# The low part of each weight tile in two pieces on GpSimd (one core, two hybrid layers with PEER experts)

## The chip, the cores and the metric

The kernel runs on one core of one Trainium2 chip. A core has five engines with an instruction stream each: TensorE (PE in the profile; its loads of weights are PEld), VectorE (DVE), ScalarE (ACT), GpSimd (POOL) and SyncE (SP). They wait for each other through semaphores. Transfers are carried out by 16 DMA engines, from queues that SyncE or GpSimd fill. The metric is the device time of one execution in microseconds; lower is better. Several runs of a kernel are compared by their median.

## The reference

Two layers of a diffusion trunk over 512 latent tokens and 256 context tokens, with 1024 channels. Each layer is a normalised and modulated mixer followed by a normalised and modulated expert stage (PEER). Layer 0 mixes by differential attention and a gated linear recurrence, layer 1 by a gated delta rule and windowed attention. After layer 0 the context is no longer needed. The expert stage of each layer matters most here:

```python
def peer_ffn(h, w_q, keys, u_tab, v_tab):          # P_HEADS 8, P_NKEYS 128, P_TOPK 16
    ...
    def block(xb):                                 # 128 tokens
        q = (xb @ w_q).reshape(P_TOKEN_BLOCK, P_HEADS, 2, P_DQ // 2)
        s = jnp.einsum('nhpd,hpkd->nhpk', q, keys).astype(jnp.float32)
        s_top, i_top = lax.top_k(s, P_TOPK)
        cand = (s_top[:, :, 0, :, None] + s_top[:, :, 1, None, :]).reshape(...)
        cand_idx = (i_top[:, :, 0, :, None] * P_NKEYS + i_top[:, :, 1, None, :]).reshape(...)
        best, pos = lax.top_k(cand, P_TOPK)
        idx = jnp.take_along_axis(cand_idx, pos, axis=-1)
        gate = jax.nn.softmax(best, axis=-1)
        u = u_tab[idx]
        v = v_tab[idx]
        act = jax.nn.gelu(jnp.einsum('nd,nhkd->nhk', xb, u).astype(jnp.float32), approximate=False)
        return jnp.einsum('nhk,nhkd->nd', (gate * act).astype(v.dtype), v)
```

The tables `u_tab` and `v_tab` have 16384 rows of 1024 numbers each per layer. Everything is computed in float32.

## The kernel before

**Products in three parts.** A float32 product is made from fp32r operands in three matmuls. Each operand x is split into a high part, a rounded copy that ScalarE makes (`activation ... Copy`, line 230), and a low part x - high (`tensor_tensor ... subtract`, line 233), on VectorE or GpSimd as the caller says. `mm3` then sums high by high (line 250), high by low (line 251) and low by high (line 253), for k = 0 to 7, one k after the other, 128 rows of the inner dimension at a time.

**Weight tiles.** `chunk` loads one weight tile of 128 x 1024 (`wraw`, 8 blocks k of 128 columns), and makes `whi` on ScalarE and `wlo` on GpSimd. A string `s.los` of letters says where the low part of the next tile is made, 'p' for GpSimd; only in the first, context stage every third one is VectorE's ('ppv', 10 tiles), everywhere else all are GpSimd's: 405 tiles, one of which has only 128 columns. The tiles are loaded ahead: `wraw` has two buffers, `whi` and `wlo` two (more in some stages).

**The stages**, in us of the profiled execution: the mixers of layer 0 and the context's retrieval to 960; the norm of layer 0's expert stage and its first query products to 1040; retrieval, expert inputs and spread of layer 0 to 1890; the sum over experts of layer 0 (`peer_out`) to 2880; layer 1's mixer to 3640; its norm and queries to 3777; retrieval, expert inputs and spread of layer 1 to 4500, of which up to 4168 mainly retrieval; `peer_out` of layer 1 to 5170; the final norm.

**Experts, dense and sparse.** Most tokens take a dense way: for each of 128 blocks j of the table, `expert_in` forms gelu(u_j . x) for all of them (matmuls `u`, lines 250, 251 and 253, with `hh` and `hl`, the parts of the normalised tokens), and `peer_out` multiplies by the gate matrix `G` and by the v rows. Ninety-six of the 128 blocks are made ahead, in `u_step` during retrieval and spread, and put aside in DRAM (`AD`); `u_step` splits its tiles two steps ahead. The last 32 are made in `peer_out`, with tiles loaded three ahead.

*Retrieval* (`retrieve`, `top`): per head two rounds of eight maxima with their indices for each of two halves, then sums of candidates `cd` (lines 1584 and 1586) and again top 16 of these, all on VectorE (lines 1553 to 1557 are the top-8 searches).

*Spread* makes the dense gate matrix: one-hot rows `ohA` (line 1685, VectorE) and `ohB` (line 1695 VectorE, 1692 and 1693 ScalarE, in turn for some tiles), a matmul `g` (line 1697) for each token, a copy `stg` to SBUF (1698) and a transfer to `G`.

*Sparse*: the remaining tokens (128 or 256 of them) get their rows by gathers. `fetch` (line 1721) is an indirect DMA that GpSimd issues, of 128 rows of 1024 numbers into a buffer `ga`; VectorE then makes a dot product (line 1733, `pu`) or a weighted sum (line 1746, `pv`) from each. There are 4 (layer 0) or 6 (layer 1) buffers, and one or two gathers are taken per step of the other work (`pull`).

**Order.** A scheduler with a timeline of its own sets the order of each engine's instructions from the program. A gather is put behind the last low part that GpSimd was given: `s.anchor` is that instruction, and `fetch` issues with `issue_after(s.anchor)`. So the low parts, the gathers and the other low parts on GpSimd (`hl` of the norm; `wl` of the gates in `peer_out`) share one queue whose order the scheduler chooses.

Of the kernel before, what the change touches and what calls it, by code (L numbers as in the profile page):

```python
# [9 lines left out]
F32 = mybir.dt.float32  # L10
# [4 lines left out]
AF = mybir.ActivationFunctionType  # L15
OP = mybir.AluOpType
# [4 lines left out]
DT = D // 128  # L21
# [186 lines left out]
class Net:  # L208
# [130 lines left out]
    def chunk(s, src):  # L339

        nc = s.nc
        r = s.t(s.next_pool(s.rps), [128, DT, 128], tag='wraw')
        up = s.next_pool(s.ups)
        hi = s.t(up, [128, DT, 128], F32R, tag='whi')
        lo = s.t(up, [128, DT, 128], F32R, tag='wlo')
        m = src.shape[2]
        nc.sync.dma_start(out=r[:, :, 0:m], in_=src)
        s.los = s.los[1:] + s.los[0]
        s.split(r[:, :, 0:m], hi[:, :, 0:m], lo[:, :, 0:m], lo_eng=nc.gpsimd if s.los[-1] == 'p' else nc.vector)
        return hi, lo  # L350


# [1714 lines left out]
```

## Time and profile before

| | |
|---|---|
| runs | 5204.75, 5197.26, 5203.47 us; median 5203.47 |
| profiled execution | 5212.4 us, its span 5210.6 us |
| busy share: PE, PEld, DVE, ACT, POOL | 86%, 70%, 77%, 39%, 53% |
| mean granted clock of TensorE | 0.92 |
| `wlo` on GpSimd (line 233) | 405 instructions, 1018.5 us busy, 2517 ns in the mean |
| waits of PE for `wlo` (line 253) | 116.2 us |
| gathers (line 1721) | 512 from `pu`, 384 from `pv`, 1313 and 1333 ns each on GpSimd |

Busy shares are means over stages with different limits. A wait is idle time of an engine that ended when the named instruction of another engine was done. "PE u L253 <- POOL wlo L233" reads: the matmul `u` of line 253 on TensorE waited for the low part `wlo` of line 233 on GpSimd.

### The profile page before, as it was taken

To read this page: it belongs to the slowest core of one execution; us is meant where nothing else is said; L and a number is where in the kernel's file an instruction comes from. 1 tells how busy PE (TensorE), PEld (TensorE's weight loads), DVE (VectorE), ACT (ScalarE), POOL (GpSimd) and SP (SyncE) were. 2 spreads that over 40 slices of the span, in tenths; PEclk is the share of its full clock that TensorE was granted. 3 is DMA by queue.
4 is the path that set the end of the run, shared out by engine and by line. 5 is a ranking of instruction groups with operands and counts; after the bars stand their busy time and mean duration, and the time that the engine had idled before them with its cause. 6 is when DMAs were issued, how large, how long until landed. Compare 5 with 4: busy or idle time off the path is not lost. (4 is left out here: it accounts for less than half of the span.)

```text
span 5210.6 us, 73804 instructions
## 1 busy us (share of the span) xinstructions
PE 4469.9 (86%) x26350; PEld 3651.6 (70%) x26350; DVE 4026.8 (77%) x7777; ACT 2019.6 (39%) x3979; POOL 2769.9 (53%) x1839
## 2 busy tenths in 40 slices
PE   7899988788889979999899898897966777799997
PEld 5777766576677867777677676785766676677775
DVE  4665568899999868888887774662699988788997
ACT  3444443234555642222222365342333553233332
POOL 2232223676557746655565320442466676587884
PEclk8899998898999989999999997898977888899999
DMA  5431124687778978887787310004367787899996
GB/s 200 145 115 60 59 77 154 196 270 239 248 264 294 321 275 298 291 296 273 279 286 274 113 51 25 6 6 145 103 219 232 254 291 266 292 343 330 356 353 218
DMA packets 453552, 1109.50 MB, mean 213 GB/s; under 512 B 40640, under 2 KB 204864, under 8 KB 449088
## 3 DMA queue, kind: packets, MB, share of 16 engines
q1 hardware_dynamic: 323872, 633.91, 36.2%
q0 software_dynamic: 129312, 470.87, 25.4%
q8 instruction: 208, 3.41, 0.3%
q14 instruction: 160, 1.31, 0.1%
HBM read 995.58 MB, written 109.05 MB: 212 GB/s over the span
## 5 line engine op out<-in xcount | busy, mean ns | idle before, releaser
L233 POOL TENSOR_TENSOR wlo<-wraw,whi 128x1024 fp32r<-128x1024 f32 x405 | 1018.5, 2517 | 1033.9 <-ACT whi L230 954.8
L1721 POOL DMA_INDIRECT ga<-in_pu,idx x512 | 672.3, 1313 | 380.9 <-DVE ga L1733 122.7
L253 PE MATMUL u<-hh,wlo 128*128 128x512 f32 (+1 forms) x2048 | 750.4, 367 | 116.2 <-POOL wlo L233 116.2
L1733 DVE SCALAR_TENSOR_TENSOR ga<-ga,htok 128x1024 f32<-128x1024 f32 x512 | 762.1, 1504 | 64.7 <-DMA ga<-in_pu,idx 64.5
L250 PE MATMUL u<-hh,whi 128*128 128x512 f32 (+1 forms) x2048 | 749.2, 366 | 45.5 <-DVE xl L1912 23.7
L251 PE MATMUL u<-hl,whi 128*128 128x512 f32 (+1 forms) x2048 | 739.9, 361 | 0.0
L230 ACT ACTIVATE whi<-wraw 128x1024 fp32r<-128x1024 f32 x415 | 436.8, 1054 | 739.2 <-PE u L251 350.8
L1746 DVE SCALAR_TENSOR_TENSOR sacc<-ga,sact,sacc 128x1024 f32<-128x1024 f32 x381 | 589.2, 1546 | 100.8 <-DMA ga<-in_pv,idx 89.0
L1721 POOL DMA_INDIRECT ga<-in_pv,idx x384 | 512.0, 1333 | 220.3 <-DVE sacc L1746 82.5
L253 PEld LDWEIGHTS u<-hh,wlo 128*128 128x128 f32 x2048 | 431.3, 211 | 164.6 <-POOL wlo L233 124.5
L250 PEld LDWEIGHTS u<-hh,whi 128*128 128x128 f32 x2048 | 431.8, 211 | 101.5 <-DVE xl L1912 34.2
L251 PEld LDWEIGHTS u<-hl,whi 128*128 128x128 f32 x2048 | 429.9, 210 | 39.2
L233 DVE TENSOR_TENSOR vl<-vraw,vh 128x768 fp32r<-128x768 f32 (+1 forms) x256 | 354.4, 1392 | 88.0 <-ACT vh L230 71.5
L1697 PE MATMUL g<-ohB,ohA 128*128 128x128 f32 x1792 | 300.7, 299 | 129.1 <-DVE ohB L1695 106.1
L1697 PEld LDWEIGHTS g<-ohB,ohA 128*128 128x128 f32 x1792 | 265.5, 205 | 176.6 <-DVE ohB L1695 76.8
L1695 DVE TENSOR_SCALAR ohB<-c_all,pt 128x128 f32<-128x128 f32 x512 | 314.4, 637 | 60.9 <-PE g L1697 60.5
L230 ACT ACTIVATE vh<-vraw 128x768 fp32r<-128x768 f32 (+1 forms) x256 | 239.6, 945 | 283.9 <-PE acc L1991 222.2
L1992 PE MATMUL acc<-wh,vl 128*128 128x512 f32 x768 | 305.9, 398 | 30.0 <-DVE vl L233 29.8
L1990 PE MATMUL acc<-wh,vh 128*128 128x512 f32 x768 | 292.8, 396 | 28.0 <-ACT wh L230 27.9
L1991 PE MATMUL acc<-wl,vh 128*128 128x512 f32 x768 | 302.5, 394 | 8.8 <-POOL wl L233 8.8
L2007 PE MATMUL acc<-vl,wh 128*128 128x512 f32 x768 | 256.6, 401 | 16.1 <-DVE vl L233 15.9
L2006 PE MATMUL acc<-vh,wh 128*128 128x512 f32 x768 | 222.5, 401 | 50.8 <-ACT vh L230 29.7
(513 smaller groups left out, 10099.2 us busy)
## 6 DMA issues: line engine op xcount, KB each, us to landing
wraw<-in_uT SPq DMA_DIRECT2D x256, 512.0 KB
vraw<-in_pv SPq DMA_DIRECT2D x256, 512.0 KB
G<-stg SPq DMA_DIRECT2D x28, 2048.0 KB
wraw<-in_ada_w SPq DMA_DIRECT2D x96, 512.0 KB
wraw<-in_ew SPq DMA_DIRECT2D x64, 512.0 KB
G<-G SPq DMA_DIRECT2D x32, 1024.0 KB
wraw<-in_pwq SPq DMA_DIRECT2D x48, 512.0 KB
AD<-act SPq DMA_DIRECT2D x96, 256.0 KB
```

Of the source, the lines that this page charges most:

```text
L230: nc.scalar.activation(hi, x, AF.Copy)
L233: i = (lo_eng or nc.vector).tensor_tensor(lo, x, hi.bitcast(F32), OP.subtract)
L250: nc.tensor.matmul(o, a, hh[:, k], start=(k == 0), stop=False)
L251: nc.tensor.matmul(o, a, hl[:, k], start=False, stop=False)
L253: nc.tensor.matmul(o, b, hh[:, k], start=False, stop=(k == nk - 1))
L1695: nc.vector.tensor_scalar(B, C['iota'], pt[:, 1, c:c + 1], pt[:, 2, c:c + 1], op0=OP.is_equal, op1=OP.mult)
L1697: nc.tensor.matmul(ps[:, n], A[:, n], B, start=True, stop=True)
L1721: nc.gpsimd.indirect_dma_start(out=ga, out_offset=None, in_=tab, in_offset=bass.IndirectOffsetOnAxis(ap=idx[:, k:k + 1], axis=0))
L1733: nc.vector.scalar_tensor_tensor(ga, ga, 1.0, htok, op0=OP.mult, op1=OP.mult, accum_out=act[:, k:k + 1])
L1746: nc.vector.scalar_tensor_tensor(acc, ga, act[:, k:k + 1], acc, op0=OP.mult, op1=OP.add)
L1991: nc.tensor.matmul(acc[d], a, wl, start=False, stop=False)
L1992: nc.tensor.matmul(acc[d], b, wh, start=False, stop=sp)
```

## The change

In `chunk`, where the low part is GpSimd's, it is made in two instructions of 4 blocks k, 512 columns each, instead of one of 8 blocks. The high part stays one instruction on ScalarE. `s.anchor` becomes the second of the two. Where the low part is VectorE's, nothing changes. Line numbers from 350 on move by 8; the new subtraction is on line 354 and its copy on 351.

```diff
--- before.py
+++ after.py
@@ -346,7 +346,15 @@
         m = src.shape[2]
         nc.sync.dma_start(out=r[:, :, 0:m], in_=src)
         s.los = s.los[1:] + s.los[0]
-        s.split(r[:, :, 0:m], hi[:, :, 0:m], lo[:, :, 0:m], lo_eng=nc.gpsimd if s.los[-1] == 'p' else nc.vector)
+        if s.los[-1] == 'p':
+
+            nc.scalar.activation(hi[:, :, 0:m], r[:, :, 0:m], AF.Copy)
+            for k in range(0, DT, DT // 2):
+                p = slice(k, k + DT // 2)
+                i = nc.gpsimd.tensor_tensor(lo[:, p, 0:m], r[:, p, 0:m], hi[:, p, 0:m].bitcast(F32), OP.subtract)
+            s.anchor = i.ins
+        else:
+            s.split(r[:, :, 0:m], hi[:, :, 0:m], lo[:, :, 0:m])
         return hi, lo
```

The order of all engines changes with it, since the scheduler gives each instruction its place. Three places follow, before and after the change; numbers in names differ by position only (`ga`: gather buffer, `wlo`: low part of a weight tile, `hl`: low part of the normalised tokens).

GpSimd at the norm of layer 0's expert stage, before the change:

```order
L1721 DMA ga_8449<-in_pu,idx_1732_8260 128x1024
L1721 DMA ga_8451<-in_pu,idx_1732_8260 128x1024
L1721 DMA ga_8453<-in_pu,idx_1732_8260 128x1024
L1721 DMA ga_8455<-in_pu,idx_1732_8260 128x1024
L233 TENSOR_TENSOR hl_8747<-h_8891,hh_8746 128x512
L233 TENSOR_TENSOR hl_8747<-h_8896,hh_8746 128x512
L233 TENSOR_TENSOR hl_8747<-h_8901,hh_8746 128x512
L1721 DMA ga_8458<-in_pu,idx_1732_8260 128x1024
L1721 DMA ga_8493<-in_pu,idx_1732_8260 128x1024
L233 TENSOR_TENSOR hl_8747<-h_8906,hh_8746 128x512
L1721 DMA ga_8496<-in_pu,idx_1732_8260 128x1024
L1721 DMA ga_8531<-in_pu,idx_1732_8260 128x1024
```

and after it:

```order
L233 TENSOR_TENSOR hl_8833<-h_8977,hh_8832 128x512
L233 TENSOR_TENSOR hl_8833<-h_8982,hh_8832 128x512
L233 TENSOR_TENSOR hl_8833<-h_8987,hh_8832 128x512
L1729 DMA ga_8528<-in_pu,idx_1732_8338 128x1024
L1729 DMA ga_8530<-in_pu,idx_1732_8338 128x1024
L1729 DMA ga_8532<-in_pu,idx_1732_8338 128x1024
L1729 DMA ga_8534<-in_pu,idx_1732_8338 128x1024
L233 TENSOR_TENSOR hl_8833<-h_8992,hh_8832 128x512
L233 TENSOR_TENSOR hl_8833<-h_8997,hh_8832 128x512
L1729 DMA ga_8537<-in_pu,idx_1732_8338 128x1024
L1729 DMA ga_8573<-in_pu,idx_1732_8338 128x1024
L1729 DMA ga_8576<-in_pu,idx_1732_8338 128x1024
```

Three `hl` now stand ahead of the four gathers that they stood behind, and the fourth `hl` stands behind four gathers instead of six.

GpSimd in the spread of layer 1, around the weight tiles 350 to 353, before the change (both pieces begin with the same gather, the 601st of the program):

```order
L1721 DMA ga_36305<-in_pu,idx_6889_33160 128x1024
L1721 DMA ga_36308<-in_pu,idx_6889_33160 128x1024
L233 TENSOR_TENSOR wlo_36596<-wraw_36594,whi_36595 128x1024
L1721 DMA ga_36372<-in_pu,idx_6889_33160 128x1024
L1721 DMA ga_36416<-in_pu,idx_6889_33160 128x1024
L233 TENSOR_TENSOR wlo_36669<-wraw_36667,whi_36668 128x1024
L1721 DMA ga_36419<-in_pu,idx_6889_33160 128x1024
L1721 DMA ga_36456<-in_pu,idx_6889_33160 128x1024
L233 TENSOR_TENSOR wlo_36745<-wraw_36743,whi_36744 128x1024
L1721 DMA ga_36514<-in_pu,idx_6889_33160 128x1024
L1721 DMA ga_36517<-in_pu,idx_6889_33160 128x1024
L233 TENSOR_TENSOR wlo_36818<-wraw_36816,whi_36817 128x1024
```

and after it ("x2" is two instructions that follow each other):

```order
L1729 DMA ga_36640<-in_pu,idx_6889_33442 128x1024
L354 TENSOR_TENSOR wlo_36936<-wraw_36934,whi_36935 128x512 x2
L1729 DMA ga_36643<-in_pu,idx_6889_33442 128x1024
L1729 DMA ga_36708<-in_pu,idx_6889_33442 128x1024
L354 TENSOR_TENSOR wlo_37010<-wraw_37008,whi_37009 128x512 x2
L1729 DMA ga_36753<-in_pu,idx_6889_33442 128x1024
L354 TENSOR_TENSOR wlo_37087<-wraw_37085,whi_37086 128x512 x2
L1729 DMA ga_36756<-in_pu,idx_6889_33442 128x1024
L1729 DMA ga_36794<-in_pu,idx_6889_33442 128x1024
L1729 DMA ga_36853<-in_pu,idx_6889_33442 128x1024
L354 TENSOR_TENSOR wlo_37161<-wraw_37159,whi_37160 128x512 x2
L1729 DMA ga_36856<-in_pu,idx_6889_33442 128x1024
```

The first `wlo` stands one gather earlier, the following ones one to two gathers earlier than before, counted from the same first gather.

TensorE in the spread of layer 1, around the weight tile 330, before the change, with what each row waits for (Pool_49 is GpSimd's semaphore):

```order
L1697 MATMUL g_34534<-ohB_34547,ohA_34535 128x128 [waits Activation_49]
L253 MATMUL u_35574<-hh_31545,wlo_35497 128x256 [waits Pool_49]
L250 MATMUL u_35574<-hh_31545,whi_35496 128x256
L251 MATMUL u_35574<-hl_31546,whi_35496 128x256
L253 MATMUL u_35574<-hh_31545,wlo_35497 128x256
```

and after it:

```order
L253 MATMUL u_35896<-hh_31806,wlo_35817 128x256 [waits Pool_49]
L250 MATMUL u_35896<-hh_31806,whi_35816 128x256
L251 MATMUL u_35896<-hl_31807,whi_35816 128x256
L253 MATMUL u_35896<-hh_31806,wlo_35817 128x256
...
L251 MATMUL u_35896<-hl_31807,whi_35816 128x256
L1705 MATMUL g_34782<-ohB_34785,ohA_34783 128x128 [waits DVE_49,Activation_49]
L1705 MATMUL g_34782<-ohB_34788,ohA_34783 128x128 [waits Activation_49]
L253 MATMUL u_35896<-hh_31806,wlo_35817 128x256 [waits Pool_49]
L250 MATMUL u_35896<-hh_31806,whi_35816 128x256
L251 MATMUL u_35896<-hl_31807,whi_35816 128x256
L253 MATMUL u_35896<-hh_31806,wlo_35817 128x256
```

There was one wait for GpSimd, at k = 0 (the first row of line 253); now there are two, at k = 0 and at k = 4, and two `g` matmuls (line 1705 after the change) stand between.

## Rows read from the trace of the kernel before

**Rows 1.** Three stretches; columns: stretch, length, busy us of PE, PEld, DVE, ACT, POOL, PEclk.

```profile
1040.00:1540.00 500.00, 428.45 (x2000) 351.02 (x1999) 490.42 (x1263) 224.66 (x458) 321.41 (x189) 0.94 0.77 254
3777.00:4168.00 391.00, 267.36 (x1723) 254.38 (x1722) 388.48 (x942) 157.00 (x311) 254.87 (x149) 0.79 0.74 235
4168.00:4500.00 332.00, 229.80 (x1435) 213.22 (x1435) 260.59 (x421) 134.07 (x271) 203.48 (x118) 0.82 0.77 269
```

**Rows 2.** GpSimd's work on wlo alone, in three stretches; x is the count of instructions.

```profile
1040.00:1540.00 500.00, 157.98 (x62) 0.94 0.77 254
3777.00:4168.00 391.00, 144.56 (x59) 0.79 0.74 235
4500.00:5170.00 670.00, 64.67 (x25) 0.98 0.95 340
```

**Rows 3.** Waits of PE, 3777 to 4168; columns: total us, times, longest us.

```profile
PE u L253 <- POOL wlo L233: 71.7, 18, 14.3
```

**Rows 4.** Waits of PE, 4168 to 4500.

```profile
PE u L253 <- POOL wlo L233: 42.4, 19, 5.8
PE g L1697 <- DVE ohB L1695: 29.1, 26, 3.0
```

**Rows 5.** Waits of DVE, 4168 to 4500.

```profile
DVE ohB L1695 <- PE g L1697: 45.3, 11, 9.1
```

**Rows 6.** Instructions of line 233 over the span: ns min/median/max, first and last start.

```profile
L233 POOL TENSOR_TENSOR wlo<-wraw,whi x405: 461/2398/3851, 40.9 to 5007.1; 128x1024 fp32r<-128x1024 f32 x135
L233 POOL TENSOR_TENSOR wl<-ad,wh x96: 1267/1297/2012, 1900.0 to 2873.8; 128x512 fp32r<-128x512 f32 x96
L233 POOL TENSOR_TENSOR wl<-G,wh x128: 986/1180/2377, 4496.2 to 5161.9; 128x384 fp32r<-128x384 f32 x128
```

**Rows 7.** Groups of DVE by line, 1040 to 1540: busy us, mean ns.

```profile
L1584 DVE TENSOR_TENSOR cd<-tv 128x64 f32<-128x64 f32 x29 | 23.0, 793 | 0.0
L1586 DVE TENSOR_TENSOR cd<-tv 128x48 f32<-128x48 f32 x29 | 11.8, 405 | 0.0
```

**Rows 8.** Groups of DVE by line, 3777 to 4168.

```profile
L1584 DVE TENSOR_TENSOR cd<-tv 128x64 f32<-128x64 f32 x20 | 23.9, 1195 | 0.0
L1586 DVE TENSOR_TENSOR cd<-tv 128x48 f32<-128x48 f32 x19 | 14.6, 766 | 0.0
```

**Rows 9.** Timeline, 3781 to 3783; columns: start us, us, engine, line.

```profile
3781.41 0.19 DVE L1586 TENSOR_TENSOR cd<-tv 128x48 f32<-128x48 f32 x1
3782.16 2.41 POOL L233 TENSOR_TENSOR wlo<-wraw,whi 128x1024 fp32r<-128x1024 f32 x1 [0.86 <-ACT whi L230]
3782.53 2.13 DVE L1584 TENSOR_TENSOR cd<-tv 128x64 f32<-128x64 f32 x1
```

**Rows 10.** Timeline, 4569 to 4574: two subtractions of GpSimd and a dot.

```profile
4569.03 2.56 POOL L233 TENSOR_TENSOR wlo<-wraw,whi 128x1024 fp32r<-128x1024 f32 x1
4569.27 3.41 DVE L1733 SCALAR_TENSOR_TENSOR ga<-ga,htok 128x1024 f32<-128x1024 f32 x1
4571.55 2.00 POOL L233 TENSOR_TENSOR wl<-G,wh 128x384 fp32r<-128x384 f32 x1
```

**Rows 11.** Timeline, 3845 to 3855, GpSimd and VectorE.

```profile
3845.74 8.40 DVE L1733 SCALAR_TENSOR_TENSOR ga<-ga,htok 128x1024 f32<-128x1024 f32 x1
3846.05 7.00 POOL L233 TENSOR_TENSOR wlo<-wraw,whi 128x1024 fp32r<-128x1024 f32 x3
```

**Rows 12.** Waits of DVE, 950 to 1000.

```profile
DVE h L305 <- POOL hl L233: 6.2, 1, 6.2
```

**Rows 13.** Timeline of GpSimd, 955 to 966.

```profile
956.27 1.11 POOL L1721 DMA_INDIRECT ga<-in_pu,idx  x1 [4.91 <-DVE idx L1711]
961.13 2.49 POOL L233 TENSOR_TENSOR hl<-h,hh 128x512 fp32r<-128x512 f32 x2
```

**Rows 14.** Timeline, 4211 to 4214.

```profile
4211.54 2.36 POOL L233 TENSOR_TENSOR wlo<-wraw,whi 128x1024 fp32r<-128x1024 f32 x1
4213.96 0.58 PE L253 MATMUL u<-hh,wlo 128*128 128x256 f32 x1 [2.21 <-POOL wlo L233]
```

## The prediction

> **What bounds the kernel now.** I read the busy time by stretches first, then the waits of TensorE and VectorE in the stretches where a low part is waited for, and last the timeline around single low parts. GpSimd itself bounds nothing: it is busy 53% of the span. Three places depend on when a low part (`wlo`) is ready, or on how long it holds up another engine.
>
> (a) The two stretches in which VectorE is the bound. From 1040 to 1540 (retrieval of layer 0) it is busy 490.42 of 500 us, from 3777 to 4168 (the same of layer 1) 388.48 of 391, while TensorE has 428.45 and 267.36 [rows 1]. TensorE does wait for `wlo` there, 71.7 us in 18 waits of layer 1 [rows 3], but those waits are bought with time that VectorE needs anyway, so shortening them ends nothing sooner. What counts is what VectorE loses to GpSimd. It loses much: the sum `cd` of 64 columns that a top-16 search begins with (L1584) takes 1195 ns in the mean from 3777 to 4168 [rows 8], and its short neighbour of 48 columns 0.19 us when nothing runs on GpSimd [rows 9]. One long `cd` begins 0.37 us into a `wlo` and ends with it: 2.13 us, from 3782.53 to 3784.66, where the `wlo` of 3782.16 ends at 3784.57 [rows 9]. So a VectorE instruction of this kind stands still until GpSimd's tensor operation is over.
>
> (b) The stretch from 4168 to 4500 (spread of layer 1). No engine is full there. TensorE waits 42.4 us in 19 waits for `wlo` and 29.1 us in 26 for the one-hot rows `ohB` of VectorE [rows 4]; VectorE in turn waits 45.3 us in 11 waits for the `g` matmuls of TensorE [rows 5]. This is a loop: VectorE frees a gather buffer, GpSimd issues the gather and then makes `wlo`, TensorE stands at the `u` matmul that needs `wlo` with `g` matmuls behind it, and VectorE waits for those. Here a low part that is usable sooner ends the stretch sooner.
>
> (c) The norm of layer 0, where VectorE waits 6.2 us once for an `hl` [rows 12], which GpSimd begins at 961.13, behind four gathers that start at 956.27 [rows 13].
>
> **The price of two pieces.** A `wlo` of 1024 columns takes 2.398 us in the median, a 512-column subtraction of the same kind (`wl<-ad`) 1.297 us [rows 6]. Two pieces: 2 x 1.297 = 2.59 us, so 0.20 us more per weight tile; by the shortest row of the 512-column form, 1.267, it is 2.53 and +0.14. I take +0.17. The first piece is ready 2.40 - 1.30 = 1.10 us sooner, the second 0.17 later. 404 tiles x 0.17 = 69 us of GpSimd's time, in the idle half of that engine except where VectorE or TensorE stands behind it.
>
> **Term 1, the norm of layer 0: -5 us.** The new order puts three `hl` ahead of the four gathers (the first place in the change's section). The wait of 6.2 us loses the 961.13 - 956.27 = 4.9 us of gathers. Bounds 0 (the gathers' later start costs it again) and -6.
>
> **Term 2, the VectorE-bound stretches: -8 us.** Stalls of `cd` now: 29 x (0.793 - 0.2) + 29 x (0.405 - 0.2) = 17 + 6 us [rows 7], and 20 x (1.195 - 0.2) + 19 x (0.766 - 0.2) = 20 + 11 us [rows 8], together 54. An add that arrives at a random moment in an operation of 2.40 us waits 1.20 in the mean, in one of two of 1.29 each 0.65: 46% less, if VectorE gets in between. After the add come the search's own steps on a single operand, which run beside GpSimd; I count four in five as so covered: -54 x 0.46 x 0.8 = -20. Against that: 62 + 59 = 121 tiles lie in these stretches [rows 2]; 54 / 1.2 = 45 of them meet an add, the other 76 meet dots and one-hot rows, of which the next one stalls on the second piece too, at 76 x 0.17 = +13. Together -7 to -8. Whether VectorE does get in between is what the trace shows with mixed answers. Of the 37 places where two subtractions of GpSimd follow each other without a gap and a dot or another blocked instruction is queued, it got in 30 times: the dot of 4569.27 ends at 4572.68, 1.1 us after the first subtraction's end at 4571.59, and the second one takes 2.00 us [rows 10] where its median is 1.18 [rows 6]. It didn't 7 times: a dot stood from 3845.74 for 8.40 us through three `wlo` [rows 11]. Bounds: -20 (no cost) and +20 (no gain, 121 x 0.17).
>
> The Trainium skill says on its page "SBUF — State Buffer", section "Who interferes with whom", that VectorE with two operands in SBUF and GpSimd reading SBUF take turns on one shared port pair, whoever starts first holding it for its whole instruction. The `cd` of [rows 9] agrees; by that rule two pieces are two holds, with a gap in which the other may take the pair.
>
> **Term 3, the spread of layer 1: -14 us.** Each of the 19 waits [rows 4] ends about 1.1 us sooner with the first piece: the row at 4213.96 waited 2.21 us for the `wlo` of 4211.54, which took 2.36 [rows 14]. In the new order TensorE waits for the first piece at k = 0 and again for the second at k = 4 (third place in the change's section), but between them are 12 matmuls, which cover the second piece. GpSimd's rows also put each `wlo` one to two gathers earlier here (second place). 19 x 1.0 us is 19; I take three quarters, since a gather that is now behind the `wlo` comes 1 to 2 us later and its dot on VectorE can be what is waited for instead. Bounds: 0 (the loop turns at the pace of the gathers) and -42 (all the waits go).
>
> **Term 4, everywhere else: +3 us.** In layer 0's other stages and in the odd mixer no `wlo` wait of TensorE stands among the long ones; the longer pieces lie beside matmuls. In the second expert stage (4500 to 5170) 25 tiles [rows 2] x 0.2 = 5 us, of which half is hidden by the weights loaded three tiles ahead. Were that cover gone, and one gather's time of 1.3 us lost at every fourth tile besides, it would be 5 + 8 = 13. Bounds 0 and +13.
>
> Sum: -5 - 8 - 14 + 3 = -24 us against the profiled execution of 5212.4, thus 5188. That execution lay 9 us above the median of the runs, 5203.5; by that ratio the forecast is **5180 us**. What can be told from no change is about 0.2%, 10 us. Own range of this case: 5160 to 5193.
>
> **Rivals.**
> *No change that can be told (0.27).* The new order changes which gathers wait, the second half gives back what the first gained, and the loop of (b) turns at the pace of its gathers: only terms 1 and part of 2 stay. For it speaks that VectorE is full in (a) and that the gather of a buffer, its landing and its dot are untouched; against it the waits of [rows 4]. -5 - 8 + 3 = -10 at most, 0 at least: 5193 to 5204, some above.
>
> *Slower (0.18).* GpSimd goes from the first piece to the second with no moment in which VectorE gets the port, as in [rows 11]. Then every tile holds VectorE 0.17 to 0.2 us longer, 121 x 0.17 to 0.2 = +21 to +24 us in (a), the gathers behind it start later, and (b) gains nothing as its gathers come late: 5203 + 22 + 3 - 5 = 5223. Term 2 turns into a loss once VectorE gets in at fewer than two in three of the borders (20 x 2/3 = 13, the cost), and the whole into one of over 10 us when it gets in at almost none and term 3 fails with it. For it: 7 of 37 cases. Against it: 30 of 37. The Trainium skill's "GPSIMD Engine Reference", section "Instruction dispatch", says that an instruction's completion doesn't hold back the next one on GpSimd. That is the rule which speaks for this rival; the trace bears it out in the 7 cases and not in the 30.
>
> *Much faster (0.12 of the 0.55).* All of the 42.4 us of [rows 4] go, since the earlier place of the `wlo` adds to the earlier first half: 5203 - 42 - 5 - 8 + 3 = 5151.
>
> That the change does nothing can be left out: every one of 404 rows of GpSimd is split.
>
> Chances: faster 0.55 (0.43 the forecast, 0.12 the larger gain), the same 0.27, slower 0.18. The range of 8 in 10 goes from the larger gain, 5150, to half way into the slower case, 5214.
>
> **What would show it.** Right: `wlo` in pieces of about 1.29 us; `cd` (L1584) with a mean from 3777 to 4168 well under 1195 ns; the wait of TensorE for `wlo` from 4168 to 4500 at about 20 to 25 us; the wait for `hl` near 960 gone. Wrong: VectorE instructions that stand through both pieces; a second `wlo` wait at k = 4; the stretch from 3777 to 4500 as long as before, with the waits renamed to `ohB` or to gathers; a longer stretch from 4500 on.

## The result, and the profile after

The changed kernel takes 5166.9 us in the median of four runs (5158.15 to 5169.19), the kernel before 5204.11 in four (5197.26 to 5206.85): a ratio of 0.9927, 95% interval 0.9911 to 0.9943, 37 us less. The forecast was 5180, the range 5150 to 5214. The profiled execution of the changed kernel is its fastest, 5158.15 us; that of the kernel before lay above its median. So the two profiles differ by 54 us where the medians differ by 37, and a stage's difference below may be scatter by some us.

The stretches of [rows 1], found again in the changed kernel by the instructions at their ends (columns as there):

```profile
1018.00:1516.00 498.00, 423.67 (x1969) 344.93 (x1969) 484.52 (x1265) 225.66 (x459) 342.86 (x250) 0.94 0.76 254
3732.00:4122.00 390.00, 254.74 (x1738) 241.62 (x1736) 385.54 (x943) 159.84 (x313) 267.57 (x208) 0.84 0.74 237
4122.00:4437.00 315.00, 217.62 (x1420) 200.67 (x1421) 265.89 (x418) 131.88 (x268) 211.45 (x157) 0.84 0.80 280
```

The two stretches that VectorE bounds are as long as before, to 2 us. The last stretch, the spread of layer 1, is 17 us shorter. TensorE's waits there, beside [rows 4], and VectorE's beside [rows 5]:

```profile
PE u L253 <- POOL wlo L354: 34.3, 19, 3.7
PE g L1705 <- DVE ohB L1703: 32.2, 32, 4.1
```

```profile
DVE ohB L1703 <- PE g L1705: 20.4, 6, 9.7
```

The wait for `wlo` fell by 8 us and VectorE's for the `g` matmuls by 25 (5.3 us of it reappear as a wait of `ohB` for a `u` matmul). The price of the pieces, beside [rows 6] (view of line 354 over the span, and the group of the 512-column form):

```profile
L354 POOL TENSOR_TENSOR wlo<-wraw,whi x810: 480/1292/2794, 41.8 to 4958.1; 128x512 fp32r<-128x512 f32 x161, 128x64 fp32r<-128x64 f32 x1
```

```profile
L354 POOL TENSOR_TENSOR wlo<-wraw,whi 128x512 fp32r<-128x512 f32 x808 | 1147.3, 1443 | 981.7 <-ACT whi L351 910.5 <-issue 23.4 <-DVE SS L783 10.8
```

The median piece takes 1.292 us, the forecast's 1.29, but the mean is 1.443: two pieces hold GpSimd 2.89 us where one took 2.52, so 0.37 more and not 0.17. Some long pieces stand behind VectorE, as the second subtraction of [rows 10] did: the piece that begins at 3765.20 takes 1.74 us, beside a `peq` of VectorE (3763.99, 1.80 us) that ends 0.59 us into it. The `cd` adds beside [rows 7] (1018 to 1516) and [rows 8] (3732 to 4122):

```profile
L1592 DVE TENSOR_TENSOR cd<-tv 128x64 f32<-128x64 f32 x29 | 21.5, 743 | 0.0
L1594 DVE TENSOR_TENSOR cd<-tv 128x48 f32<-128x48 f32 x29 | 12.4, 429 | 0.0
...
L1592 DVE TENSOR_TENSOR cd<-tv 128x64 f32<-128x64 f32 x19 | 13.8, 728 | 0.0
L1594 DVE TENSOR_TENSOR cd<-tv 128x48 f32<-128x48 f32 x19 | 9.4, 496 | 0.0
```

Their stalls are 16 + 7 + 10 + 6 = 38 us by the sum of term 2, where they were 54 (52 without the 20th `cd` of [rows 8], as 19 stand in the stretch now). The timeline has both ways that a border between pieces can go. VectorE gets in at 3776 (`ind` ends 0.13 us after the first piece, which ended at 3776.26), and doesn't at 3862, where a `cd` stands through four pieces of two tiles:

```profile
3774.96 2.60 POOL L354 TENSOR_TENSOR wlo<-wraw,whi 128x512 fp32r<-128x512 f32 x2 [0.21 <-ACT whi L351]
3775.13 1.26 DVE L1642 TENSOR_TENSOR ind<-peq 128x64 f32<-128x64 bf16 x1
...
3862.14 4.99 POOL L354 TENSOR_TENSOR wlo<-wraw,whi 128x512 fp32r<-128x512 f32 x4
3862.41 4.81 DVE L1592 TENSOR_TENSOR cd<-tv 128x64 f32<-128x64 f32 x1
```

Counted over the whole trace, in the way that gave 30 of 37 before, VectorE gets in at 127 of 230 borders. In the two stretches that VectorE bounds it gets in at only about four in ten of some 90. Of the 37 borders of before, four lie in these two stretches, and it got in at none of them; [rows 11] has two of the four.

**Where the time went, stage by stage.** The program is the same but for the pieces, so each VectorE and ScalarE group (line, operation, tiles) with equal counts in two traces gives the difference of its ends; the median of these in steps of 10 us says how far one kernel is ahead at each place. The table has what each stage gained or lost (us, named by the times of before), for the change and for the experiments that follow:

```
run               0-340  -840 -1040 -1540 -1890 -2880 -3780 -4170 -4500 -5160
changed kernel     -3.0 -16.6  -6.6  +0.7  -0.6 -16.5  -3.7  +1.7 -16.7  +5.0
e1_spread1         +3.7  -2.7  -2.0  +5.1  -1.1  +4.7 -15.0  -1.7 -24.5  +8.4
e2_mix0            +3.1 -13.6  -5.9  +1.7  -0.9 -11.2  +1.3  +0.2 -11.0  -1.6
e3_peer0           -1.2  +1.3  -1.3  -1.8   0.0 -20.6  +1.2  +1.8  +0.9  -1.7
e4_reversed        -2.7  +8.7  -2.8  +7.2  -2.9 -21.1  -0.5  +4.8 -11.9  -2.3
e5_one_tile        -0.5  +0.1  -2.6  +0.2  -0.2 -13.7  -5.6  +6.8  -7.5  -3.3
e6_tile5           -5.1  +1.1  -2.1  -2.2  -0.9  +3.3  +2.4  -0.7  -9.9  -2.2
e7_tile8           -0.3  +5.1  -1.0  +1.9  -0.7  +0.5  -0.8  +0.1  +0.6  -1.4
e8_one_and_seven   -3.1  -8.8  -6.6  +3.5  -0.8  +2.1 -13.2  -3.3  -9.3  -2.3
e9_old_order       -2.6  +0.7  -1.0  +1.1  -0.8  +1.0  +0.2  +0.5  -7.8  -1.2
e10_mixers_spread  -3.8 -13.8  -6.9  +2.2   0.0 -18.9 -28.5  -6.1  -9.0  -2.5
e11_four_pieces   -15.8 -16.6 -14.4  +6.7  +0.2 -25.8 -15.9  -4.5 -16.0 +17.4
e12_tile17         +0.2  -0.1  +3.7  -3.6  -2.6  +8.5  +0.3  +0.9  -1.3  -7.1
```

A row is one execution of each kernel, and the place of a border matters. e10 has the changed kernel's pieces in the retrieval and spread of layer 1 and, but for a few rows, GpSimd's order there; it gained 6.1 and 9.0 us in these two stages, where the changed kernel lost 1.7 and gained 16.7. Their sum is 15.1 and 15.0, so it is safer to read the two together.

Three stages carry the change's gain: layer 0's mixers (to 840), the sum over experts of layer 0 (1890 to 2880) and the spread of layer 1 (4170 to 4500). Only the last was in the forecast with a gain of this size.

### The profile page after: what moved, and what is told of

Read it like the earlier page. It is cut to its first block, busy times and chain, and to the rows that moved or that the text cites. A ratio compares the mean times of both kernels' runs of the same rounds, so it can differ in the third digit from the quotient of the medians.

```text
span 5156.4 us, 74375 instructions
## 1 busy us (share of the span) xinstructions
PE 4427.5 (86%) x26350; PEld 3625.3 (70%) x26350; DVE 3975.7 (77%) x7777; ACT 2022.6 (39%) x3979; POOL 2888.2 (56%) x2244
## 5 line engine op out<-in xcount | busy, mean ns | idle before, releaser
L354 POOL TENSOR_TENSOR wlo<-wraw,whi 128x512 fp32r<-128x512 f32 x810 | 1148.4, 1441 | 982.1 <-ACT whi L351 910.8
L1741 DVE SCALAR_TENSOR_TENSOR ga<-ga,htok 128x1024 f32<-128x1024 f32 x512 | 742.6, 1464 | 94.0 <-DMA ga<-in_pu,idx 93.6
L351 ACT ACTIVATE whi<-wraw 128x1024 fp32r<-128x1024 f32 x405 | 426.2, 1054 | 748.4 <-PE u L251 361.0
L1754 DVE SCALAR_TENSOR_TENSOR sacc<-ga,sact,sacc 128x1024 f32<-128x1024 f32 x381 | 563.7, 1480 | 112.0 <-DMA ga<-in_pv,idx 107.4
```

Of the source, the lines that this page charges most:

```text
L351: nc.scalar.activation(hi[:, :, 0:m], r[:, :, 0:m], AF.Copy)
L354: i = nc.gpsimd.tensor_tensor(lo[:, p, 0:m], r[:, p, 0:m], hi[:, p, 0:m].bitcast(F32), OP.subtract)
L1741: nc.vector.scalar_tensor_tensor(ga, ga, 1.0, htok, op0=OP.mult, op1=OP.mult, accum_out=act[:, k:k + 1])
L1754: nc.vector.scalar_tensor_tensor(acc, ga, act[:, k:k + 1], acc, op0=OP.mult, op1=OP.add)
```

## The experiments

All but the changed kernel itself use one form of `chunk`, in which a letter of `LOS` says how a tile's low part is made. `LOS` has one string for each stage: the context; layer 0's mixers; its retrieval and spread; layer 1's mixer; its retrieval and spread; the sums over experts of layer 0 and of layer 1. Lines move by some numbers from run to run: 257 is the matmul of line 253, 237 the subtraction of line 233, and 357 to 362 stand where the changed kernel has 351 and 354. The code is shortened here:

```diff
+PIECES = {'h': [k 0-3, k 4-7], 'r': [k 4-7, k 0-3], 'q': [k 0-1, k 2-3, k 4-5, k 6-7]}
-        s.split(..., lo_eng=nc.gpsimd if s.los[-1] == 'p' else nc.vector)
+        if how in 'pv':
+            s.split(..., lo_eng=nc.gpsimd if how == 'p' else nc.vector)
+        else:
+            nc.scalar.activation(hi[:, :, 0:m], r[:, :, 0:m], AF.Copy)
+            for ks, cs in PIECES[how](m):
+                i = nc.gpsimd.tensor_tensor(lo[:, ks, cs], ...)
+            s.anchor = i.ins
```

Two theories were on trial. *Pieces*: time is saved because the first piece is ready sooner, or because VectorE gets the port between pieces. *Order*: time is saved because the scheduler, given other durations, draws another order, which it also does in stages where nothing is in pieces. Each group of experiments is compared with runs of the kernel before on the same chip.

**One stage at a time, and the pieces turned round** (5 to 12 runs each, against 29 of before, median 5210.35).

```diff
-LOS = 'ppv,p,p,p,p,p,p'.split(',')
+LOS = 'ppv,p,p,p,h,p,p'.split(',')     # e1_spread1
+LOS = 'hhv,h,p,p,p,p,p'.split(',')     # e2_mix0
+LOS = 'ppv,p,h,p,p,h,p'.split(',')     # e3_peer0
+LOS = 'rrv,r,r,r,r,r,r'.split(',')     # e4_reversed
```

> Two pieces only for the weight tiles of layer 1's expert stage before its sum over experts (retrieval, expert inputs and spread); all others in one. First-piece theory (TensorE starts on k = 0 to 3 while the second piece is made): the whole gain of term 3 is here, -14 to -17 us, so 5187 to 5190, with TensorE's wait for wlo in the spread of layer 1 near 34 us as in the changed kernel and the stretch about 15 us shorter. Rival (the gain came from the new order of layer 0's mixer): within 5 us of 5204.

> Two pieces only for the weight tiles of layer 0's mixers and the context's expert stage, up to 960 us. The comparison of the two profiles says -24 to -27 us for this stretch, so 5177 to 5180. First-piece theory as predicted (nothing waits for wlo there): 5200 to 5207, and the 27 us of the profiles are due to something else, the scatter of executions (5158 to 5169 for the changed kernel) among it.

> Two pieces only for the weight tiles of layer 0's expert stage, its sum over experts included, 960 to 2880 us. Comparison of the two profiles: +5 in the norm, -2 and -2 in retrieval and spread, -16 in the sum over experts, so about -15 and 5189. First-piece theory as predicted: -5 for the norm and the first part of term 2, -4: about 5195. Rival (VectorE pays for longer holds of the port): 5206 to 5215.

> Two pieces everywhere, but the piece with k = 4 to 7 is made first, so that TensorE's k = 0 waits for both; the price of two instructions, and the moment between them in which VectorE can get the port, stay. First-piece theory: term 3 goes into a loss, 42 us of waits become 19 x 0.2 = 4 longer, and the total is 5200 to 5210. Port theory (what counts is that VectorE gets in between): nearly the gain of the change, 5165 to 5180.

Measured: e1 0.9965 (0.9952 to 0.9978), e2 0.9930 (0.9913 to 0.9947), e3 0.9968 (0.9954 to 0.9982), e4 0.9968 (0.9952 to 0.9984), so 18, 36, 17 and 17 us less. e4's 5191 us lie between its two forecasts. The three parts e1, e2 and e3 sum to 71 us, twice the whole. The table says why: e2 gains 11 us in the sum over experts of layer 0 and 11 in the spread of layer 1, and has no piece in either. It has another order there. And e4, where TensorE's first matmul has to wait for both pieces, gains 12 us in that spread all the same, 7 with the retrieval ahead of it. The waits of TensorE for `wlo` in the spread, e2 first, then e4:

```profile
PE u L257 <- POOL wlo L237: 32.5, 16, 5.4
```

```profile
PE u L257 <- POOL wlo L359: 33.1, 16, 4.8
```

Both are as low as the changed kernel's. A first piece that is ready sooner isn't needed to lower the wait this far.

**One tile in pieces, or none that matters** (10 to 12 runs each, against 33 of before, median 5213.23).

```diff
+        s.nch = getattr(s, 'nch', 0) + 1
+        if how == 'p' and s.nch == 1:          # e5_one_tile; 5: e6_tile5; 8: e7_tile8; 17: e12_tile17
+            how = 'h'
```

```diff
+PIECES = [k 0, k 1-7]                          # e8_one_and_seven, every tile
```

> Only the first of the 405 weight tiles is made in two pieces; every other tile is made in one, as before. Its direct cost is 0.2 us at the very start. The scheduler answers by another order in the sum over experts of layer 0 (there it is the changed kernel's, row for row on GpSimd) and in layer 1's retrieval and spread. Piece theory (time comes from the pieces themselves): within 5 us of before. Order theory (the new order is what pays): about -15 us from the sum over experts of layer 0, as the two profiles gave, and -10 or so more, or less, in layer 1; 5180 to 5195.

> Only the fifth weight tile is made in two pieces. The order of everything up to layer 1's spread stays that of before; from the middle of layer 1's spread on it is the order of the run with pieces in layer 0's mixers alone, which had no pieces there either. Order theory: TensorE's wait for wlo from 4170 to 4500 falls from 42 to about 33 us, and this stretch is about 11 us shorter, as in that run; total -8 to -12. Piece theory: no change, the stretch 330 us, the wait 42 us.

> Only the eighth weight tile is made in two pieces, and the order of every engine stays that of before but for one row. Both theories: within 5 us of before; it says what the repeated timing of one order can differ by.

> Every tile on GpSimd is made in two pieces, the first of them only k = 0 (128 columns), the second k = 1 to 7. The first piece is ready some 1.9 us sooner than the whole was, but TensorE needs the second about 0.4 us later, which is 0.2 us later than the whole was. In the sum over experts of layer 0 the order is that of before. Piece theory: gains of the first piece small, total near before, 5200 to 5215. Order theory: no gain in the sum over experts of layer 0, and whatever the orders of layer 0's mixers and layer 1's spread give, so between -20 and +5 us.

Measured: e5 0.9958 (0.9944 to 0.9973), e6 0.9983 (0.9964 to 1.0003), e7 1.0009 (0.9990 to 1.0027), e8 0.9942 (0.9923 to 0.9962). e8, 30 us less, gained more than either of its expectations had it; 13 us of it stand in layer 1's mixer, which neither had named. One tile of 405 in two pieces makes the kernel 22 us faster, by the order that follows from it: 14 us of it in the sum over experts of layer 0, where the rows of GpSimd stand as in the changed kernel. The seven kernels with that order there (e11 but for two rows) gained 11 to 26 us in this stage, the three without a piece in it (e2, e5, e10) 11 to 19; the six with the order of before are between +0.5 and +8.5, e8 among them, which has its pieces there. In that stage the order gives the gain; what halves would add under the order of before was not run. The trace shows what the order changes: VectorE's instructions of the stage, the same 905, take it less time, 776 to 782 us in the seven kernels and 791 to 797 in the six (906 of them in e12). The stretch in the kernel before, then in e5:

```profile
1890.00:2880.00 990.00, 905.73 (x3778) 720.27 (x3778) 797.07 (x905) 265.72 (x444) 589.85 (x426) 0.97 0.80 288
```

```profile
1887.00:2863.00 976.00, 901.55 (x3776) 721.14 (x3777) 777.95 (x905) 265.77 (x444) 586.77 (x426) 0.97 0.82 292
```

In the spread, e6 (no piece near it, GpSimd's order that of e2) is 10 us shorter, with a wait for `wlo` of 30 us, though its whole time can't be told from no change (TensorE's waits, then VectorE's):

```profile
PE u L257 <- POOL wlo L237: 30.2, 13, 5.5
```

```profile
DVE ohB L1709 <- PE g L1711: 27.3, 4, 8.1
```

The control e7 is where it should be in the whole; in the mixers the same order took 5.1 us more. The repeated spread with the old order and no pieces (e3, e7, e12) is 331, 331 and 329 us against 330, so for one order that stage can be read to 1 or 2 us.

**Pieces with GpSimd's old order, and more of them** (5 to 12 runs each, against 17 of before, median 5207.56).

```diff
+        if how == 'p' and s.nch in (353, 354, 355, ..., 391, 392):   # e9: 27 of the spread's 40 tiles
+            how = 'h'
```

```diff
+LOS = 'hhv,h,p,p,h,p,p'.split(',')     # e10_mixers_and_spread
+LOS = 'qqv,q,q,q,q,q,q'.split(',')     # e11_four_pieces
```

> Pieces without a new order: 27 of the 40 weight tiles of layer 1's spread, chosen so that GpSimd's order stays that of before row for row, and TensorE's but for some 50 places of a few rows each; all other tiles in one. First-piece theory (term 3): 27/40 of 19 waits end 1.1 us sooner, so the stretch from 4170 to 4500 goes from 330 to about 317 to 322 us, the wait for wlo from 42 to about 30, and the total falls by 8 to 13. Order theory: the stretch stays at 329 to 332 us, the wait within 4 us of 42, the total within 5 us of before.

> Pieces in layer 0's mixers and in layer 1's retrieval and spread, where the runs with pieces in one stage alone gained; everything else in one, with the order of the changed kernel in the sum over experts of layer 0. If the gains add: -12 to -20 (mixers), -14 (sum over experts, by its order), -11 to -24 (spread), +8 (second sum over experts): -30 to -50, so 5155 to 5175, as fast as the changed kernel or a little faster. If each stage's gain is that of whatever order the scheduler draws, it can lie anywhere from 5165 to 5205.

> Every tile on GpSimd in four pieces of 256 columns. By the 256-column subtractions (0.72 to 0.74 us) a tile costs 2.9 us in place of 2.4, the first piece is ready 1.7 us sooner. First-piece theory: a larger gain in layer 1's spread than with two pieces, 300 to 308 us for the stretch. Port theory: VectorE's stretches 1040 to 1540 and 3777 to 4168 get shorter still, as an add waits for 0.36 us in the mean; against it the cost of 121 x 0.5 = 60 us, half of it unseen. Order theory: these stretches grow by 5 to 15 us for the dearer tiles, and the rest is the draw of the order.

Measured: e9 0.9988 (0.9971 to 1.0004), e10 0.9901 (0.9874 to 0.9928), e11 0.9872 (0.9850 to 0.9893). e9 is the nearest to a clean test of term 3: the spread is 7.8 us shorter with GpSimd's order unchanged, and every other stage is within 3 us. So the pieces save time without a new order of GpSimd, at 27 of 40 tiles nearly what the first-piece theory said. Two limits: TensorE's order does change in some 50 places, so part of it may be the place of the `g` matmuls; and the gain is read from one execution, as the whole time of e9 can't be told from no change. And the wait doesn't show the gain. e9's two rows for `wlo` (its pieces, then whole tiles), VectorE's wait and the whole stretch:

```profile
PE u L257 <- POOL wlo L362: 32.9, 15, 5.3
...
PE u L257 <- POOL wlo L237: 10.9, 5, 3.3
```

```profile
DVE ohB L1709 <- PE g L1711: 36.2, 8, 8.7
```

```profile
4169.00:4491.00 322.00, 219.99 (x1421) 203.17 (x1420) 260.47 (x417) 132.64 (x268) 205.10 (x142) 0.83 0.78 274
```

32.9 + 10.9 = 43.8 us of waits, against 42.4 [rows 4]. What fell is TensorE's busy time, from 229.80 [rows 1] to 219.99 us for nearly as many matmuls (1435 and 1421), at a granted clock of 0.83 in place of 0.82, and VectorE's wait for it, from 45.3 [rows 5] to 36.2. The control e7, whole tiles in the old order, has 228.37 us for 1418 matmuls:

```profile
4175.00:4505.00 330.00, 228.37 (x1418) 211.59 (x1419) 260.05 (x417) 132.08 (x267) 200.87 (x117) 0.81 0.76 268
```

e11 is the fastest, 5139.4 us in the median, and its ratio lies clear below the changed kernel's; e10 follows with 5155.3, and its interval overlaps the changed kernel's. (The profiled execution of e10 lies 28 us below its median.) Of e11's expectations the 300 to 308 us for the spread didn't come, it is 314; a tile cost 4 x 0.93 = 3.7 us of GpSimd, not 2.9. The stretches that VectorE bounds move by +6.7 and -4.5 us, though there the port theory holds for VectorE itself: the `cd` of 64 columns take 276 and 331 ns, where they took 793 [rows 7] and 1195 [rows 8]. The first stretch ends no sooner because VectorE, busy 467 of 507 us, now waits for gathers, 37.3 us in place of 6.8; GpSimd, which issues them, is busy 396 us there in place of 321 [rows 1] (group of line 359 over the span; the stretch; `cd` in it; VectorE's wait; that of before):

```profile
L359 POOL TENSOR_TENSOR wlo<-wraw,whi 128x256 fp32r<-128x256 f32 x1616 | 1460.0, 934 | 841.5 <-ACT whi L357 789.1 <-issue 17.7 <-ACT pT L1551 10.0
993.00:1500.00 507.00, 433.42 (x2005) 353.51 (x2003) 466.77 (x1273) 225.09 (x462) 396.18 (x381) 0.93 0.76 255
L1595 DVE TENSOR_TENSOR cd<-tv 128x64 f32<-128x64 f32 x29 | 8.0, 276 | 0.0
DVE ga L1744 <- DMA ga<-in_pu,idx: 37.3, 23, 4.4
```

```profile
DVE ga L1733 <- DMA ga<-in_pu,idx: 6.8, 6, 2.6
```

The second sum over experts loses 17 us. What of e11's further gain is piece and what is order was not taken apart.

**One tile in the mixers' own stage** (e12, the diff above with 17).

> Only the 17th weight tile is made in two pieces. From the sum over experts of layer 0 on, GpSimd's order is that of before; in a part of layer 0's mixers (TensorE's rows 1800 to 2300 of 18232) it becomes that of the changed kernel. Order theory for the mixers: the stretch 340 to 840 gets shorter by 5 to 14 us, since the dip of TensorE's granted clock between 520 and 560 us (0.86 and 0.80) goes, as it did in the changed kernel; total -5 to -14. Piece theory for the mixers (the many early first pieces keep TensorE busy and its clock up): this stretch stays within 5 us of 500, the dip stays, the total is within 6 us of before.

Measured: 1.0026 (1.0010 to 1.0041), and the stretch 340 to 840 is as long as before, its clock as low. The output of e12 lies off the reference's by a relative 0.028, and why is open, so nothing rests on its whole time; its stages stand above only beside those of other runs with the same order. This is one order of many, and at most it says that the gain in the mixers isn't got by this part of the order.

## Why the prediction was right, and where it was not

The sign was right and the time fell into the range, in part by luck. In the two profiles, which differ by 54 us, terms 1 and 3 came in the size that was forecast; term 2 gave +2.4 for -8, and term 4 about -35 for +3. Two thirds of the gain came from where nothing had been looked for.

*Term 1, the norm of layer 0 (-5).* The stretch 840 to 1040 gained 6.6 us. The wait of VectorE for `hl` is gone, as forecast; GpSimd's rows, beside [rows 13]:

```profile
926.90 2.87 POOL L233 TENSOR_TENSOR hl<-h,hh 128x512 fp32r<-128x512 f32 x2 [2.63 <-ACT hh L230]
934.38 1.52 POOL L233 TENSOR_TENSOR hl<-h,hh 128x512 fp32r<-128x512 f32 x1 [4.61 <-ACT hh L230]
936.07 1.11 POOL L1729 DMA_INDIRECT ga<-in_pu,idx  x1 [0.17 <-issue]
...
940.91 2.50 POOL L233 TENSOR_TENSOR hl<-h,hh 128x512 fp32r<-128x512 f32 x2
```

Three `hl` stand ahead of the four gathers, as the order said. It is the order that does it: e2, whose pieces lie before this stretch, has the same three `hl` in front, no wait, and gained 5.9; e3, which has its pieces in the stretch and the `hl` where they were, gained 1.3 and keeps the wait:

```profile
DVE h L309 <- POOL hl L237: 6.3, 1, 6.3
```

*Term 2, the VectorE-bound stretches (-8).* Measured +0.7 and +1.7. The step that failed is the share of borders at which VectorE gets in. I took it from 30 of 37 cases and counted nearly all. Those 30 lie in other stages; in these two it got in at none of four before, and at about four in ten now, fewer than the two in three at which the prediction has the term turn into a loss. The saving on `cd` came in part (14 to 16 us, forecast 20). Against it, `wlo` took GpSimd 37 us more in the two stretches, 179.42 and 159.75 us in place of 157.98 and 144.56 [rows 2], where 121 x 0.17 = 21 had been counted:

```profile
1018.00:1516.00 498.00, 179.42 (x122) 0.94 0.76 254
3732.00:4122.00 390.00, 159.75 (x119) 0.84 0.74 237
```

Part of the stall only moved to other instructions of VectorE. In layer 1's stretch (before, then after):

```profile
L1633 DVE TENSOR_TENSOR peq<-peq 128x512 bf16<-128x512 bf16 (+2 forms) x48 | 23.7, 493 | 0.1
L1711 DVE SCALAR_TENSOR_TENSOR idx<-ind,ind 128x128 int32<-128x128 f32 x2 | 0.5, 270 | 0.0
```

```profile
L1641 DVE TENSOR_TENSOR peq<-peq 128x512 bf16<-128x512 bf16 (+2 forms) x48 | 28.6, 596 | 0.2
L1719 DVE SCALAR_TENSOR_TENSOR idx<-ind,ind 128x128 int32<-128x128 f32 x2 | 5.6, 2820 | 0.0
```

By the Trainium skill, "SBUF — State Buffer", section "Who interferes with whom", an operation that takes the shared ports holds them for its whole length and the other engine waits. The long pieces (up to 2.794 us for a median of 1.292) agree: the waiting goes both ways here.

*Term 3, the spread of layer 1 (-14).* Measured -16.7, so the size was right. Its cause was told by half. With the retrieval ahead of it the changed kernel gained 15.0 us; the order that e2 and e6 share gives 11 without a piece, pieces with GpSimd's old order 7 for 27 of 40 tiles (e9), and e5's order nothing (+6.8 and -7.5). What the changed kernel's own order gives without pieces no run shows. The forecast said that the wait of TensorE would fall to 20 to 25 us; it fell to 34, and what else fell is the time TensorE is busy.

*Term 4, everywhere else (+3).* This is the term that was missed: the mixers gained 16.6 us, the sum over experts of layer 0 16.5, and the second one lost 5 (its bounds were 0 and +13). The step that failed is to have costed only waits for `wlo`, and the new order only at the places where I had looked at it. For the sum over experts the runs settle it: the order. For the mixers they don't settle it. Kernels with a first piece made first gained 8.8 to 16.6 us there, in three orders (one that the changed kernel, e2 and e10 share, and those of e8 and e11); those with one piece there at most are between -2.7 and +5.1, and e4, whose pieces are turned round and whose order is another again, lost 8.7. That fits the pieces, but no run had pieces in the mixers with the order of before, or one of these orders without pieces, so the order isn't excluded as the cause. What the time is made of there can be read; the stretch of before, the changed kernel, e4:

```profile
340.00:840.00 500.00, 458.54 (x2565) 349.66 (x2564) 307.95 (x828) 215.00 (x442) 133.87 (x70) 0.93 0.25 78
```

```profile
337.00:820.00 483.00, 443.94 (x2559) 339.71 (x2558) 300.10 (x826) 217.41 (x441) 140.03 (x116) 0.96 0.25 81
```

```profile
337.00:846.00 509.00, 463.25 (x2561) 352.34 (x2561) 303.31 (x828) 216.50 (x442) 143.09 (x116) 0.92 0.24 76
```

TensorE is busy 92% of it, with the same matmuls but for a few at the edges, and the stretch is shorter by what TensorE's busy time is (14.6 of 17 us), at a granted clock of 0.96 in place of 0.93.

Of the rivals, "slower" did not come, though its mechanism is there at 103 of 230 borders. "No change" is excluded by the interval. "Much faster" asked for all 42 us of waits for `wlo` to go; 8 went.

## What to carry to other kernels

When a scheduler sets the order, a change of an instruction's size is two changes, its length and the order of all else, and the second may weigh as much: one tile in 405 gave 22 us. Before a gain is put down to an edit, run the edit on one place that can't matter, and run it with the order held (e9), and compare stage by stage. A share that a forecast rests on (30 of 37) must be counted in the stage that it is used for. And where TensorE is nearly full, look at its busy time and clock, not at its waits alone.

## What the hardware showed that I had not expected

The granted clock makes time by itself, also where nothing was changed. In layer 1's mixer e1 runs the same instructions in the same order as the kernel before; yet the stretch that begins at 3200 in before and 3207 in e1 takes 60 us in the one and 45 in the other (rows of before, then e1, each with some 20 us ahead of it):

```profile
3180.00:3200.00 20.00, 15.80 (x84) 12.03 (x82) 9.18 (x28) 12.57 (x30) 0.00 (x0) 0.92 0.11 41
3200.00:3260.00 60.00, 52.30 (x170) 37.46 (x170) 16.86 (x58) 25.40 (x61) 0.00 (x0) 0.50 0.01 5
```

```profile
3189.00:3207.00 18.00, 14.86 (x73) 11.19 (x71) 8.55 (x24) 11.45 (x26) 0.00 (x0) 0.91 0.12 44
3207.00:3252.00 45.00, 35.95 (x173) 26.36 (x174) 17.05 (x60) 25.53 (x63) 0.00 (x0) 0.81 0.02 7
```

About 170 matmuls took 52.30 us at 0.50 (1.2 GHz) and 35.95 at a mean of 0.81. TensorE had been busy 79% and 83% of the time just before. Such a dip is worth 15 us in one execution, which is as much as most stages of this change moved; what sets it off can't be told from these rows. It makes up the -15.0 of layer 1's mixer in e1's row of the table; in e10's, -28.5 stands there, also without a piece in that stage, but TensorE's order differs.
